# A running log-sum-exp: row sums in fp32 on GpSimd and VectorE, one fp32 triangular matmul, and a carry moved by a shuffle

## The chip, the cores and the metric

The kernel runs on one core of one Trainium2 chip. The metric is the device time of one execution in microseconds. The time before the change is 1263.03 us, the median of 10 runs that lie between 1262.51 and 1263.69.

## The reference

The input `x` has shape (4, 4096, 4128) in fp32: four batches, 4096 rows in time, 4128 independent columns. The output is the running log-sum-exp along the rows:

```
out[:, 0, :] = x[:, 0, :]
for t in range(1, S):
    mx = maximum(out[:, t - 1, :], x[:, t, :])
    out[:, t, :] = mx + log(exp(out[:, t - 1, :] - mx) + exp(x[:, t, :] - mx))
```

Both kernels compute the same thing without the maximum: the exponential of every element, a running sum over the rows of a batch, and the logarithm of that sum. Every element is read once and written once, 270.53 MB each way.

## The kernel before, in words

**Tiles.** A batch of 4096 rows is cut into steps (class `Step`) of 128 x 3 = 384 rows, with one step of 256 rows over; in batch 0 that small step comes first, in the others last. There are 44 steps, numbered 0 to 43 here: 40 of three rows a partition, 4 of two. In a step, partition p holds r = 3 (or 2) consecutive rows next to each other, so a tile `xt` is [128, r, 4128] fp32. Four such buffers exist (`bufs = 4`).

**Chunks.** Each tile is cut into four chunks of 1024 columns (class `Chunk`); the last chunk of a tile also takes the 32 columns that remain, the tail.

**What a chunk does.** `exp` (L128, ScalarE) writes the exponentials as fp16 over the tile itself. `head` (matmuls, all at L88, TensorE) fills a PSUM tile `pt` of [128, 1024]: for row 0 of each partition it multiplies with the triangular matrix `incl` (own partition and all above), for the rows 1 and 2 with `excl` (all partitions above), and it adds the running sum of the tiles before with `pick` from an fp16 carry tile that has a high and a low part. The PSUM now holds the sums for row 0. `stage(j)` takes the logarithm of `pt` into row j of the tile (L162, ScalarE) and then adds row j + 1 with two more matmuls against `ident`. After the last row `keep` (L92 and L93, VectorE) copies the last quadrant of `pt` as high and low fp16 parts into the carry of this chunk. The tail has its own PSUM tile `qt`, its own matmuls and one logarithm (L167).

**What sets the order.** The order is written out by hand (`manual_schedule`): each engine does its instructions in the order in which the program issues them. Round g of the main loop issues stage 2 of chunk g-2, stage 1 of chunk g-1 and stage 0 of chunk g, then the exponential of chunk g+2 and the head of chunk g+1. So ScalarE's queue holds the exponentials of the next tile ahead of the last logarithms of the present one. When the last stage of a tile's last chunk is issued, the store of the tile goes on SyncE's queue (L116), and behind it the load (L113) of the tile three steps ahead (`ahead = bufs - 1`). That load goes into the buffer of the tile before the one stored, and waits for that tile's store to have landed. Ahead of the loop three loads are issued.

Of the kernel before, what the change touches and what calls it, by code (L numbers as in the profile page):

```python
# [6 lines left out]

FP32 = mybir.dt.float32
FP16 = mybir.dt.float16
ACT = mybir.ActivationFunctionType  # L10
P = 128
R = 3
CH = 1024
MM = 512
HI, LO = 96, 32


def _constants(nc, pool):


    def tri(base, name):
        t = pool.tile([P, P], FP16, name=name)
        nc.gpsimd.memset(t, 1.0)

        nc.gpsimd.affine_select(  # L25
            out=t, in_=t, pattern=[[1, P]], compare_op=mybir.AluOpType.is_ge,
            fill=0.0, base=base, channel_multiplier=-1,
        )
        return t

    def ones_where_zero(bases, step, name):
        t = pool.tile([P, P], FP16, name=name)
        nc.gpsimd.memset(t, 0.0)
        for base in bases:
            nc.gpsimd.affine_select(  # L35
                out=t, in_=t, pattern=[[step, P]], compare_op=mybir.AluOpType.not_equal,
                fill=1.0, base=base, channel_multiplier=1,
            )
        return t

    return (
        tri(0, "incl"),
        tri(-1, "excl"),
        ones_where_zero([0], -1, "ident"),
        ones_where_zero([-(HI + 31), -(LO + 31)], 0, "pick"),
    )


@with_exitstack
def kernel(  # L50
    ctx: ExitStack,
    tc: tile.TileContext,
    x: bass.AP,
    out: bass.AP,
):

    nc = tc.nc
    B, S, D = x.shape
    assert S % P == 0
    n_main = D // CH
    tail = D - n_main * CH
    t0 = n_main * CH
    last = n_main - 1

    nc.scalar.preload_act_table_set("natural_log_exp_and_others")  # L70
    consts = ctx.enter_context(tc.tile_pool(name="consts", bufs=1))
    incl, excl, ident, pick = _constants(nc, consts)

    bufs = 4
    xpool = ctx.enter_context(tc.tile_pool(name="xpool", bufs=bufs))
    cpool = ctx.enter_context(tc.tile_pool(name="cpool", bufs=1))
    pmain = ctx.enter_context(tc.tile_pool(name="pmain", bufs=3, space=bass.MemoryType.PSUM))
    ptail = ctx.enter_context(tc.tile_pool(name="ptail", bufs=2, space=bass.MemoryType.PSUM))

    carry = [cpool.tile([P, CH], FP16, name=f"carry{c}") for c in range(n_main)]  # L80
    carry_t = cpool.tile([P, tail], FP16, name="carry_t")
    for t in (*carry, carry_t):
        nc.vector.memset(t, 0.0)  # L83

    ctx.enter_context(tc.manual_schedule())

    def mm(pt, w, rhs, start=False, stop=False):
        nc.tensor.matmul(pt, lhsT=w, rhs=rhs, start=start, stop=stop, skip_group_check=True)  # L88

    def keep(cr, pt):  # L90

        nc.vector.tensor_copy(cr[HI:HI + 32, :], pt[HI:HI + 32])  # L92
        nc.vector.tensor_tensor(  # L93
            out=cr[LO:LO + 32, :], in0=pt[HI:HI + 32], in1=cr[HI:HI + 32, :],
            op=mybir.AluOpType.subtract,
        )

    class Step:


        def __init__(self, b, row, r):
            self.b, self.row, self.r = b, row, r
            self.first = row == 0

        def dram(self, t):
            rows = t[self.b, self.row:self.row + P * self.r, :]
            return rows.rearrange("(p j) d -> p j d", j=self.r)

        def load(self):
            full = xpool.tile([P, R, D], FP32, name="xt")  # L110
            self.xt = full[:, :self.r, :]
            self.half = self.xt.bitcast(FP16)
            nc.sync.dma_start(out=self.xt, in_=self.dram(x))  # L113

        def store(self):
            nc.sync.dma_start(out=self.dram(out), in_=self.xt)  # L116

    class Chunk:
        def __init__(self, step, c):
            self.t, self.c = step, c  # L120
            self.w = D - last * CH if c == last else CH

        def e(self, j, a, b):
            return self.t.half[:, j, 2 * self.c * CH + a:2 * self.c * CH + b]

        def exp(self):
            c0, w = self.c * CH, self.w
            nc.scalar.activation(  # L128
                self.t.half[:, :, 2 * c0:2 * c0 + w], self.t.xt[:, :, c0:c0 + w], ACT.Exp,
            )  # L130

        def head(self):
            t = self.t
            pt = self.pt = pmain.tile([P, CH], FP32, name="pt")
            for j in range(t.r):
                for s in range(0, CH, MM):
                    mm(pt[:, s:s + MM], excl if j else incl, self.e(j, s, s + MM), start=j == 0)
            if not t.first:
                for s in range(0, CH, MM):
                    mm(pt[:, s:s + MM], pick, carry[self.c][:, s:s + MM])  # L140
            if self.c == last:
                self.tail_head()

        def tail_head(self):


            t, r = self.t, self.t.r
            full = ptail.tile([P, R, tail], FP32, name="qt")
            qt = self.qt = full[:, :r, :]
            to = lambda v, n: v.unsqueeze(1).to_broadcast([P, n, tail])  # L150
            for i in range(r):
                e = self.e(i, CH, CH + tail)
                mm(qt[:, i:, :], incl, to(e, r - i), start=i == 0)
                if i:
                    mm(qt[:, :i, :], excl, to(e, i))
            if not t.first:
                mm(qt, pick, to(carry_t, r))

        def stage(self, j):

            t, c, pt = self.t, self.c, self.pt
            nc.scalar.activation(t.xt[:, j, c * CH:(c + 1) * CH], pt, ACT.Ln)  # L162
            if j + 1 < t.r:
                for s in range(0, CH, MM):
                    mm(pt[:, s:s + MM], ident, self.e(j + 1, s, s + MM), stop=j + 2 == t.r)
                if c == last and j == 0:
                    nc.scalar.activation(t.xt[:, :, t0:D], self.qt, ACT.Ln)  # L167
                    keep(carry_t, self.qt[:, t.r - 1, :])
            else:
                keep(carry[c], pt)  # L170

    steps = []
    for b in range(B):
        n = S // P
        parts = [R] * (n // R) + ([n % R] if n % R else [])
        if b == 0:
            parts.reverse()
        row = 0
        for r in parts:
            steps.append(Step(b, row, r))  # L180
            row += P * r
        assert row == S

    chunks = [Chunk(s, c) for s in steps for c in range(n_main)]
    ahead = bufs - 1
    for s in steps[:ahead]:
        s.load()
    stored = 0
    chunks[0].exp()
    chunks[1].exp()  # L190
    chunks[0].head()
    for g in range(len(chunks) + R - 1):
        for d in range(R - 1, -1, -1):
            if 0 <= g - d < len(chunks) and d < chunks[g - d].t.r:
                k = chunks[g - d]
                k.stage(d)
                if k.c == last and d + 1 == k.t.r:
                    k.t.store()
                    if stored + ahead < len(steps):
                        steps[stored + ahead].load()  # L200
                    stored += 1
        if g + 2 < len(chunks):
            chunks[g + 2].exp()
        if g + 1 < len(chunks):
            chunks[g + 1].head()


# [28 lines left out]
```

## Time and profile before

| | |
|---|---|
| median of 10 runs | 1263.03 us |
| the profiled execution, its own time | 1262.96 us |
| its span | 1261.2 us |
| ScalarE busy | 947.1 us |
| TensorE matmuls busy | 690.2 us |
| VectorE busy | 451.4 us |
| GpSimd busy | 2.2 us |
| load of a three-row tile (6192 KB), issue to landing, median | 42.2 us |
| store of a three-row tile, issue to landing, median | 28.0 us |
| mean granted TensorE clock | 0.772 |

The page gives for each group of instructions the line, the engine (PE is TensorE, DVE is VectorE, ACT is ScalarE, POOL is GpSimd, SP is SyncE), the operation, what is written from what, the count, and then the busy time with the mean of one, and the idle time of the engine ahead of it with what ended that. A timeline row has start, duration, engine, line, and the idle time before it in brackets. A busy engine is not a bound in itself: what counts is which wait ends last in a stage.

### The profile page before, as it was taken

To read this page: it belongs to the slowest core of one execution; us is meant where nothing else is said; L and a number is where in the kernel's file an instruction comes from. 1 tells how busy PE (TensorE), PEld (TensorE's weight loads), DVE (VectorE), ACT (ScalarE), POOL (GpSimd) and SP (SyncE) were. 2 spreads that over 40 slices of the span, in tenths; PEclk is the share of its full clock that TensorE was granted. 3 is DMA by queue.
4 is the path that set the end of the run, shared out by engine and by line. 5 is a ranking of instruction groups with operands and counts; after the bars stand their busy time and mean duration, and the time that the engine had idled before them with its cause. 6 is when DMAs were issued, how large, how long until landed. Compare 5 with 4: busy or idle time off the path is not lost.

```text
span 1261.2 us, 6165 instructions
## 1 busy us (share of the span) xinstructions
PE 690.2 (55%) x2268; PEld 236.3 (19%) x2268; DVE 451.4 (36%) x445; ACT 947.1 (75%) x733; POOL 2.2 (0%) x13
## 2 busy tenths in 40 slices
PE   3665554556565555565346555555535765555552
PEld 1222111112121121221112121111211221111110
DVE  2443333333333333334424333333442433333344
ACT  5997777777777777778569777777966977777794
POOL 0000000000000000000000000000000000000000
PEclk9997777777677777777768777787776777778786
DMA  9999999999999999999999999999999999999998
GB/s 411 410 435 436 428 427 436 434 430 430 436 437 429 434 435 433 430 430 436 436 428 436 434 431 434 437 430 432 435 430 435 435 430 430 436 434 432 433 422 350
DMA packets 12702, 541.46 MB, mean 429 GB/s; under 512 B 1408, under 2 KB 1408, under 8 KB 1408
## 3 DMA queue, kind: packets, MB, share of 16 engines
q1 hardware_dynamic: 12672, 541.07, 99.5%
q8 instruction: 18, 0.29, 0.1%
q14 instruction: 12, 0.10, 0.0%
HBM read 270.53 MB, written 270.53 MB: 429 GB/s over the span
## 4 chain that ended last, share of the span: by engine, by line
DMA 69%; ACT 22%; PE 5%; issue 2%; DVE 1%; SPq 0%; ACTq 0%
DMA xt<-in_x_dram 67%; ACT xt L128 11%; ACT xt L162 10%; PE pt L88 5%; DMA out_dram<-xt 2%; ACT xt L167 0%; SPq L116 0%; DVE carry L92 0%; DVE carry L93 0%; ACTq L231 0%; SPq L113 0%; ACTq L128 0%; PE qt L88 0%
## 5 line engine op out<-in xcount | busy, mean ns | idle before, releaser
L128 ACT ACTIVATE xt<-xt 128x3072 f16<-128x3072 f32 (+3 forms) x176 | 478.3, 2717 | 248.1 <-DMA xt<-in_x_dram 248.1
L88 PE MATMUL pt<-xt,ident 128*128 128x512 f16 x672 | 250.7, 470 | 529.3 <-ACT xt L162 529.2
L162 ACT ACTIVATE xt<-pt 128x1024 f32<-128x1024 f32 x512 | 487.5, 1029 | 2.5 <-PE pt L88 0.7
L92 DVE CAST carry<-pt 32x1024 f16<-32x1024 f32 x176 | 216.4, 1230 | 761.3 <-ACT xt L162 761.0
L88 PE MATMUL pt<-xt,excl 128*128 128x512 f16 x672 | 247.0, 504 | 0.0
L93 DVE TENSOR_TENSOR carry<-pt,carry 32x1024 f16<-32x1024 f32 x176 | 215.8, 1226 | 6.1
L88 PEld LDWEIGHTS <-ident 128*128 128x128 f16 x672 | 70.3, 105 | 677.0 <-issue 653.3
L88 PE MATMUL pt<-xt,incl 128*128 128x512 f16 x352 | 151.8, 525 | 23.8 <-ACT xt L128 15.1
L88 PEld LDWEIGHTS <-excl 128*128 128x128 f16 x756 | 91.8, 123 | 141.3 <-issue 108.6
L88 PE MATMUL pt<-carry,pick 128*128 128x512 f16 x320 | 111.7, 436 | 0.0
L88 PEld LDWEIGHTS <-incl 128*128 128x128 f16 x480 | 45.2, 111 | 131.3 <-DVE carry L93 95.1
L88 PEld LDWEIGHTS <-pick 128*128 128x128 f16 x360 | 40.5, 113 | 56.8 <-issue 33.9
L167 ACT ACTIVATE xt<-qt 128x96 f32<-128x96 f32 (+1 forms) x44 | 10.9, 248 | 45.9 <-PE pt L88 45.9
L92 DVE CAST carry_t<-qt 32x32 f16<-32x32 f32 x44 | 8.7, 197 | 25.5 <-ACT xt L167 25.3
L88 PE MATMUL qt<-xt,incl 128*128 128x64 f16 (+2 forms) x128 | 12.7, 199 | 0.0
L88 PE MATMUL qt<-xt,excl 128*128 128x64 f16 (+1 forms) x84 | 10.7, 188 | 0.0
L93 DVE TENSOR_TENSOR carry_t<-qt,carry_t 32x32 f16<-32x32 f32 x44 | 8.5, 193 | 1.5
L88 PE MATMUL qt<-carry_t,pick 128*128 128x96 f16 (+1 forms) x40 | 8.3, 207 | 0.0
L83 DVE MEMSET carry<- 128x512 uint32 x4 | 1.9, 485 | 1.1 <-PEq L220 1.0
L70 ACT ACT_TABLE_LOAD x1 | 1.3, 1283 | 0.8 <-PEq L220 0.8
L35 POOL TENSOR_SCALAR_AFFINE_SELECT pick<-pick 128x128 f16<-128x128 f16 x2 | 0.6, 292 | 0.1
L25 POOL TENSOR_SCALAR_AFFINE_SELECT incl<-incl 128x128 f16<-128x128 f16 x1 | 0.3, 292 | 0.0
(11 smaller groups left out, 1.9 us busy)
## 6 DMA issues: line engine op xcount, KB each, us to landing
xt<-in_x_dram SPq DMA_DIRECT2D x40, 6192.0 KB, 42.2
out_dram<-xt SPq DMA_DIRECT2D x40, 6192.0 KB, 28.0
xt<-in_x_dram SPq DMA_DIRECT2D x4, 4128.0 KB, 37.2
out_dram<-xt SPq DMA_DIRECT2D x4, 4128.0 KB, 22.9
```

Of the source, the lines that this page charges most:

```text
L25: nc.gpsimd.affine_select(out=t, in_=t, pattern=[[1, P]], compare_op=mybir.AluOpType.is_ge, fill=0.0, base=base, channel_multiplier=-1,)
L35: nc.gpsimd.affine_select(out=t, in_=t, pattern=[[step, P]], compare_op=mybir.AluOpType.not_equal, fill=1.0, base=base, channel_multiplier=1,)
L70: nc.scalar.preload_act_table_set("natural_log_exp_and_others")
L83: nc.vector.memset(t, 0.0)
L88: nc.tensor.matmul(pt, lhsT=w, rhs=rhs, start=start, stop=stop, skip_group_check=True)
L92: nc.vector.tensor_copy(cr[HI:HI + 32, :], pt[HI:HI + 32])
L93: nc.vector.tensor_tensor(out=cr[LO:LO + 32, :], in0=pt[HI:HI + 32], in1=cr[HI:HI + 32, :], op=mybir.AluOpType.subtract,)
L128: nc.scalar.activation(self.t.half[:, :, 2 * c0:2 * c0 + w], self.t.xt[:, :, c0:c0 + w], ACT.Exp,)
L162: nc.scalar.activation(t.xt[:, j, c * CH:(c + 1) * CH], pt, ACT.Ln)
L167: nc.scalar.activation(t.xt[:, :, t0:D], self.qt, ACT.Ln)
```

## The change

All fp16 goes; everything is fp32 and stays in the tile. A chunk of a tile of r rows is now done so:

- `act(Exp)`: the exponential over the chunk's r rows, in place (ScalarE).
- `begin` (except in a batch's first tile): VectorE adds the carry, the running sum of all tiles before, to row 0 of partition 0. The instruction covers 32 partitions and multiplies the carry by `one`, which is 1 in partition 0 and 0 in the other 31.
- `own`: GpSimd adds row j-1 to row j in each partition, r - 1 instructions. (The change's own words give this sum to VectorE; the code issues it on `nc.gpsimd`.) Afterwards the last row of a partition holds the sum of its rows.
- `head`: two fp32 matmuls of 512 columns (and one of 32 for the tail) of the last row with `excl` give in PSUM, for each partition, the sum over all partitions above it.
- `add_before`: one VectorE instruction adds that PSUM tile to all r rows (a broadcast); one more does the tail.
- `end` (except in a batch's last tile): a VectorE `stream_shuffle` copies partition 127's last row of the chunk into all 32 partitions of the carry. The carry of chunk 0 lies in PSUM, those of the chunks 1 to 3 in SBUF.
- `act(Ln)`: the logarithm over the r rows with the tail, in place (ScalarE).

Round g issues the exponential of chunk g+3, `begin` and `own` of g+2, `head` of g+1, the logarithm of chunk g-1, then `add_before` and `end` of chunk g. The store of a tile follows its last logarithm. Four loads are issued ahead of the loop; the first store brings no load, and from the second store on each store is followed by the load three steps ahead, as before. The last step is a loop of its own, so none of its instructions is issued before all of the other 43 steps are. `hpool` holds two PSUM tiles for `head` (three `pt` before).

```diff
+    excl = pool.tile([P, P], FP32, name="excl")
...
+    one = pool.tile([Q, 1], FP32, name="one")
...
+    carry = [psum.tile([Q, CH], FP32, name="carry0")]
+    carry += [cpool.tile([Q, CH if c < last else D - last * CH], FP32, name=f"carry{c}")
+              for c in range(1, NC)]
...
+    def add(eng, o, a, b):
+        eng.tensor_tensor(out=o, in0=a, in1=b, op=mybir.AluOpType.add)
...
+        def act(self, func):
+            v = self.t.xt[:, :, self.a:self.b]
+            nc.scalar.activation(v, v, func)
+
+        def begin(self):
+
+            t = self.t
+            if not t.first:
+                v = t.xt[:Q, 0, self.a:self.b]
+                nc.vector.scalar_tensor_tensor(
+                    out=v, in0=carry[self.c], scalar=one, in1=v,
+                    op0=mybir.AluOpType.mult, op1=mybir.AluOpType.add,
+                )
+
+        def own(self):
+
+            x = self.t.xt
+            for j in range(1, self.t.r):
+                v = x[:, j, self.a:self.b]
+                add(nc.gpsimd, v, x[:, j - 1, self.a:self.b], v)
 
         def head(self):
...
+            e = t.xt[:, t.r - 1, self.a:self.b]
+            self.pt = hpool.tile([P, CH], FP32, name="pt")
+            parts = [(self.pt[:, s:s + MM], e[:, s:s + MM]) for s in range(0, CH, MM)]
             if self.c == last:
...
+                self.qt = psum.tile([P, tail], FP32, name="qt")
+                parts.append((self.qt, e[:, CH:]))
+            for o, v in parts:
+                nc.tensor.matmul(o, lhsT=excl, rhs=v, start=True, stop=True)
+
+        def add_before(self):
+            t = self.t
+            parts = [(t.xt[:, :, self.a:self.a + CH], self.pt)]
+            if self.c == last:
+                parts.append((t.xt[:, :, t0:], self.qt))
+            for v, p in parts:
+                add(nc.vector, v, v, p.unsqueeze(1).to_broadcast(v.shape))
+
+        def end(self):
+            t = self.t
+            if not t.final:
+                nc.vector.stream_shuffle(
+                    carry[self.c], t.xt[P - Q:, t.r - 1, self.a:self.b], [Q - 1] * Q,
+                )
...
-    for s in steps[:ahead]:
+    for s in steps[:bufs]:
         s.load()
     stored = 0
...
+    def result(k):
+        nonlocal stored
+        k.act(ACT.Ln)
+        if k.c == last:
+            k.t.store()
+            if bufs <= stored + ahead < len(steps):
+                steps[stored + ahead].load()
+            stored += 1
+
+
+    for part in (steps[:-1], steps[-1:]):
+        chunks = [Chunk(s, c) for s in part for c in range(NC)]
+        N = len(chunks)
+        for g in range(-3, N + 1):
+            if 0 <= g + 3 < N:
+                chunks[g + 3].act(ACT.Exp)
+            if 0 <= g + 2 < N:
+                chunks[g + 2].begin()
+                chunks[g + 2].own()
+            if 0 <= g + 1 < N:
+                chunks[g + 1].head()
+            if 0 <= g - 1:
+                result(chunks[g - 1])
+            if 0 <= g < N:
+                chunks[g].add_before()
+                chunks[g].end()
```

## The prediction

> **What bounds the kernel now.** I read the page first: busy shares, slices, queues, chain.
>
> ```profile
> span 1261.2 us, 6165 instructions
> PE 690.2 (55%) x2268; PEld 236.3 (19%) x2268; DVE 451.4 (36%) x445; ACT 947.1 (75%) x733; POOL 2.2 (0%) x13
> ...
> DMA  9999999999999999999999999999999999999998
> ...
> q1 hardware_dynamic: 12672, 541.07, 99.5%
> ...
> DMA 69%; ACT 22%; PE 5%; issue 2%; DVE 1%; SPq 0%; ACTq 0%
> ```
>
> The 16 DMA engines are full in every slice but the last; no compute engine passes 75%. The chain is loads (67%) joined by short pieces of ScalarE. So the transfers set the pace, and a change can cost time only by letting the DMA run dry. How far is it from that? SyncE's timeline of two tiles, then ScalarE's and SyncE's at the end (the last row merges three stores, issued at 1212.2, 1233.8 and 1244.4):
>
> ```profile
> 722.71 0.34 SPq L116 DMA_DIRECT2D out_dram<-xt  x1
> 723.14 0.38 SPq L113 DMA_DIRECT2D xt<-in_x_dram  x1
> 751.95 0.34 SPq L116 DMA_DIRECT2D out_dram<-xt  x1
> ```
>
> ```profile
> 1196.39 2.76 ACT L128 ACTIVATE xt<-xt 128x3072 f16<-128x3072 f32 x1 [6.16 <-DMA xt<-in_x_dram]
> ...
> 1220.98 1.91 ACT L128 ACTIVATE xt<-xt 128x2048 f16<-128x2048 f32 x1 [1.34 <-DMA xt<-in_x_dram]
> ```
>
> ```profile
> 1182.81 0.34 SPq L116 DMA_DIRECT2D out_dram<-xt  x1
> 1183.25 0.38 SPq L113 DMA_DIRECT2D xt<-in_x_dram  x1
> 1212.22 32.54 SPq L116 DMA_DIRECT2D out_dram<-xt  x3
> ```
>
> A three-row tile takes 29.3 us (722.7 to 752.0): one load and one store at 14.65 us each. ScalarE waits 6.2 us for tile 42 (landed 1196.4), and tile 41's store goes out 15.8 us later, at 1212.2, because ScalarE's queue holds three exps of tile 42 ahead of tile 41's last logs. I call this delay, landing of the next tile to store, L. At landing only one load (14.65 us, issued with the previous store) and that store are still queued, 29.3 us of work; so with L = 15.8 us about 13.5 us of cover remain, and the DMA runs dry in mid-run only if L exceeds 29.3 us.
>
> The costs of single instructions:
>
> ```profile
> L128 ACT ACTIVATE xt<-xt 128x3072 f16<-128x3072 f32 x120 | 332.0, 2767 | 233.3 <-DMA xt<-in_x_dram 233.3
> L128 ACT ACTIVATE xt<-xt 128x3168 f16<-128x3168 f32 x40 | 115.5, 2886 | 0.0
> L128 ACT ACTIVATE xt<-xt 128x2048 f16<-128x2048 f32 x12 | 22.9, 1912 | 14.8 <-DMA xt<-in_x_dram 14.8
> ```
>
> ```profile
> L93 DVE TENSOR_TENSOR carry<-pt,carry 32x1024 f16<-32x1024 f32 x176 | 215.8, 1226 | 6.1
> L93 DVE TENSOR_TENSOR carry_t<-qt,carry_t 32x32 f16<-32x32 f32 x44 | 8.5, 193 | 1.5
> ```
>
> VectorE: (1226 - 193) / 992 = 1.04 ns an element after 160 ns.
>
> **What the Trainium skill says.** "VectorE: DVE Perf Modes", the perf-mode tier table: an fp32 tensor_tensor has no faster mode, 2293 ns for 2048 elements, and a shuffle of [32, 2048] about 2400 ns. My line gives 2290 ns: the trace agrees. "GPSIMD Engine Reference", 3.1: a GpSimd fp32 add of 2048 takes 4497 ns; no row of this trace shows one. "SBUF — State Buffer", Who interferes with whom: a VectorE instruction with two SBUF inputs and a GpSimd one that reads SBUF lock each other out for whole instructions; one with a PSUM input does not. Nothing here shows it. "FP8 and Floating Point Precision", TensorE Precision Notes: true fp32 is four passes; not shown here.
>
> **The change part by part,** for a three-row tile, against 29.3 us.
>
> *ScalarE.* Four exps as before. The logs, twelve from PSUM at 1.029 us, become four over 3072 or 3168 elements; I price them like the exps: 2.77. Exps and logs together: 2 x (3 x 2.77 + 2.89) = 22.4 us. Beside the transfers, except in L.
>
> *VectorE.* `keep` goes (two at 1.23 a chunk). `begin` adds 1.23, `end` 1.25 (the shuffle), `add_before` 3072 elements: 0.16 + 3072 x 1.04 ns = 3.36, and 0.26 for the tail. A tile: 4 x 5.84 + 0.3 = 23.7, about 24 with gaps; bounds 23 and 26. Whole run some 980 us. Covered; if the cover went, the tile would take these 24 us plus what it waits for. The set-up memsets that go (1.9 us) lay before the first landing: nothing.
>
> *GpSimd.* `own`: two adds of 1024 a chunk. The page's 4497 ns less 0.1 fixed (its one-element memset takes 98 ns here) halves to 2.2, plus 0.1: 2.3 us. From below, the trace's one-input select of 128 elements (292 ns) gives 1.5 ns an element, 1.6 us; from above I allow 3.3. `begin` reads the carry from SBUF in three of four chunks, and is locked against `own`; `own` in turn waits for its `begin`. So they alternate: 1.23 + 2 x 2.3 + two hand-overs of 0.1 = 6.0 us a chunk, 24 a tile. Behind a waiting `begin` on VectorE stand `add_before` and `end` (4.6 us), which fit beside the next `own` (4.6). Covered, with 5 us left.
>
> *TensorE.* Twelve 512-column matmuls a chunk fall to two, nine matmuls a tile with the tail (should the 18 in the change's words count halves, the work is the same). In the last tile, two pairs:
>
> ```profile
> 1233.61 1.06 PE L88 MATMUL pt<-carry,pick 128*128 128x512 f16 x2
> ...
> 1239.60 0.59 PE L88 MATMUL pt<-xt,ident 128*128 128x512 f16 x2 [1.75 <-ACT xt L162]
> ```
>
> A single one takes 378 ns where a pair takes 0.59 us, so a second pass adds 0.21; the slower granted clock gives 0.63 and 1.06, so 0.43. The page's four passes for each of two matmuls make eight: 1.9 to 3.6 us a head. I take 2.6. Covered in mid-run.
>
> *Order of the queues, mid-run.* In round g ScalarE does exp(g+3), then log(g-1). Tile k's last log now stands behind all four exps of tile k+1: L = four exps and four logs = 22.4 us. VectorE's `begin` of tile k+1 also blocks `add_before` of tile k's third chunk until the first exp; then 2.8 + 1.2 + 3.4 = 7.4 us after landing, well before the log that needs it (11). So L = 22.5 and cover falls from 13.5 to 6.8 us. It costs nothing while L stays below 29.3; the next load waits for the previous store on SyncE's queue, which lands some 7 us before. Cost: 0 (bounds 0 and +3, since the 16 engines don't run level: from 1230 to 1235 us they moved 211 GB/s, a part of them dry before store 42 came).
>
> *Start.* Four loads are issued at once, but no load goes with store 0. Loads land at 13.2, 27.8, and by 14.65 steps 42.4 and 57.1; store 0 (9.8 us) would end at 66.9. ScalarE reaches store 0 four rounds after tile 1's landing, 27.8 + 4 x 4.75 = 46.8 (exp 2.8, log 1.95), and store 1 four full rounds later, 69.2. A transfer into an empty queue costs more: the first load took 13.18 - 0.80 = 12.4 for 9.8 of work, so 2.6. The queue is dry for 69.2 + 2.6 - 66.9 = 4.9 us; fast engines are dry sooner, slow ones later. Before, store 1 (63.7) and load 3 met no gap. I take +4 (bounds 0 and +10, the latter with GpSimd adds of 2.9).
>
> *End.* The last tile is now a pipeline of its own: its first exp stands behind tile 42's last log. Tile 42 lands at 1196.4 + 4 = 1200.4. Its fourth `begin` ends some 22 us after landing (2.8 for the first exp, three rounds of 6, its own 1.2); VectorE still has three `add_before` and two `end`: 3 x 3.36 + 0.3 + 2 x 1.25 = 12.9, so 35, less the 0.8 by which the first rounds run ahead of 6; the last log ends at 37 and store 42 goes at 1237.5 (before: 1233.8). Then exp 1.9, begin 1.2, one GpSimd add 2.3, head 2.6, add_before 2.3, log 1.9 and hand-overs 0.4 make 12.6 us to the first chunk's result, three more at 3.7 and a tail 0.3: 24 us, store 43 at 1261.5 (before 1244.4). Store 42 ends 17 us after its issue, so the queue is dry about 8 us. The last store needs 9.8 + 2.6 = 12.4: landing 1273.9, and 0.8 to the end of the span as now: 1274.7. Bounds on this part: last tile 20 to 28, drain 32 to 41.
>
> **Sum.** 1261.2 + 4 (start) + 0 (mid-run) + 9.5 (end) = 1274.7 of span; 1.8 lies around the span (1262.96 - 1261.2), so 1276.5. That execution is 0.07 us from the median of 1263.03. Forecast: 1276, its own range 1267 to 1288.
>
> **Rivals.** (A) *GpSimd and the lock become the pace.* Decides at an add of (29.3 / 4 - 1.23 - 0.2) / 2 = 2.95 us. At 3.3 a chunk takes 8.0 us, a full tile 32, and 40 full tiles 1280, four small ones 19 each and 30 of fill and drain: about 1385. For it: no row shows the price. Against: the stated price has 28% to spare. (B) *Not slower.* The dry spell at the start falls into slack of the slow engines (cost 0), and a last tile of 19 us after a drain of 31 us brings the last store out at 1196.4 + 31 + 19 = 1246.4, end 1246.4 + 12.4 + 0.8 + 1.8 = 1261.4. It decides if GpSimd's add is nearer 1.6 and TensorE's head 1.9 us. Against: the last tile starts only after the drain, whatever the adds cost. (C) *The words rather than the diff*: with the row sums on VectorE, 8 x 1.23 more a tile is 33.5 us; 40 x 33.5 and four small tiles of 24, with fill and drain, some 1450. The diff has them on GpSimd.
>
> **Chances.** Forecast 0.70, A 0.17, B 0.11, C 0.02. The range leaves out the upper part of A, C and the lower part of B: 1262 to 1310. About 0.2% (1260.5 to 1265.6) is what a measurement of this kernel can tell from no change: faster 0.05, same 0.07, slower 0.88.
>
> **What would show it.** DMA slices still full in mid-run, with one dip near 65 to 72 us and one of 8 us before the last store; ScalarE idle at every landing, stores 22 to 23 us after it; GpSimd adds of 2.2 to 2.4 us; VectorE near 980 us. If ScalarE no longer waits for loads, or GpSimd's adds pass 2.9 us, A holds and I am wrong; if store 1 leaves before 66 us, the start term is.

## The result, and the profile after

The changed kernel takes 1293.59 us (median of 8 runs, 1292.55 to 1295.46), against 1262.96 us before: ratio 1.0245, 95% interval 1.0237 to 1.0254. It is 30.6 us slower; the forecast had 13. The profiled execution, the fastest of them, took 1292.55 us with a span of 1290.4.

The page of the changed kernel, the lines that answer to those shown of before:

```profile
span 1290.4 us, 3961 instructions
PE 607.3 (47%) x792; PEld 212.1 (16%) x792; DVE 990.9 (77%) x700; ACT 920.9 (71%) x353; POOL 799.9 (62%) x344
...
q1 hardware_dynamic: 12672, 541.07, 98.1%
...
DMA 54%; ACT 23%; DVE 12%; issue 8%; POOL 1%; PE 1%; SPq 1%; ACTq 0%; DVEq 0%
```

Still no compute engine is full, and the same 541.07 MB move. But the DMA's share fell from 99.5% to 98.1%, and its share of the chain from 69% to 54%.

The groups of the changed kernel, shapes apart (count, then busy time and mean ns of one, then the idle time before them):

```profile
L107 ACT ACTIVATE xt<-xt 128x3072 f32<-128x3072 f32 x240 | 643.2, 2750 | 328.4 <-DMA xt<-in_x_dram 320.9 <-DVE carry L149 7.5
L136 PE MATMUL pt<-xt,excl 128*128 128x512 f32 x704 | 597.7, 1000 | 666.7 <-POOL xt L78 658.0 <-DVE xt L78 8.5 <-issue 0.2
L78 POOL TENSOR_TENSOR xt<-xt 128x1024 f32<-128x1024 f32 x252 | 596.1, 2367 | 419.6 <-DVE xt L114 366.0 <-ACT xt L107 44.2
L78 DVE TENSOR_TENSOR xt<-xt,pt 128x3072 f32<-128x3072 f32 x160 | 533.5, 3335 | 40.9 <-PE pt L136 32.1 <-issue 8.7
L114 DVE SCALAR_TENSOR_TENSOR xt<-carry,one,xt 32x1024 f32<-32x1024 f32 x120 | 159.1, 1327 | 209.0 <-ACT xt L107 206.4
L149 DVE STREAM_SHUFFLE carry<-xt 32x1024 f32<-32x1024 f32 x120 | 152.4, 1270 | 1.6
```

Most durations are near their forecasts: logarithms and exponentials 2.75 us (forecast 2.77), GpSimd's adds 2.37 (2.3), `add_before` 3.34 (3.36), the shuffle 1.27 (1.25), `begin` 1.33 (1.23). The matmuls appear as two records each of 1.0 us, 18 a tile. One price is off: the four records of a head take 3.7 us from the first start to the last end (median of 176), where 2.6 was forecast with 3.6 as the upper bound. TensorE waits 658 us for GpSimd and is off the path in mid-run, so it is not a price of an engine's work that failed.

Where did the time go? I take as a tile's landing the start of its first exponential, where ScalarE's timeline shows it waiting for the load. Tile 4 lands at 100.24 us before and 103.39 after; tile 42 at 1196.39 and 1215.95. That cuts the extra 29.2 us of span in three:

| part | before | after | more | forecast |
|---|---|---|---|---|
| start, to the landing of tile 4 | 100.2 | 103.4 | 3.2 | 4 |
| mid-run, landing of tile 4 to that of tile 42 | 1096.2 | 1112.6 | 16.4 | 0 |
| end, from there to the end of the span | 64.8 | 74.5 | 9.6 | 9.5 |

Start and end came as forecast; mid-run lost what was to cost nothing. The landing of tile 41 on ScalarE and the store of tile 40 on SyncE, in the changed kernel:

```profile
1186.65 21.50 ACT L107 ACTIVATE xt<-xt 128x3072 f32<-128x3072 f32 x8 [7.67 <-DMA xt<-in_x_dram]
```

```profile
1208.17 0.33 SPq L98 DMA_DIRECT2D out_dram<-xt  x1
1208.60 0.38 SPq L95 DMA_DIRECT2D xt<-in_x_dram  x1
```

The store follows the landing by 21.5 us (15.8 before, forecast 22.5): eight activations. The changed kernel in stretches of 3 us around the two-row tile 21 (from the left: the length, then the busy times of PE, PEld (weight loads), DVE, ACT and POOL, the granted clock, and last the DMA share and GB/s; a packet counts whole where it starts, so a full stretch can show 0.94 or 1.02):

```profile
591.00:594.00 3.00, 3.00 (x4) 0.93 (x4) 3.00 (x2) 3.00 (x2) 1.95 (x1) 0.51 1.02 440
594.00:597.00 3.00, 0.41 (x2) 0.10 (x1) 2.91 (x4) 3.00 (x2) 2.77 (x2) 1.00 0.46 198
597.00:600.00 3.00, 3.00 (x4) 0.86 (x4) 3.00 (x2) 0.23 (x1) 1.96 (x1) 0.56 0.99 424
678.00:681.00 3.00, 2.81 (x4) 0.67 (x2) 3.00 (x2) 3.00 (x3) 2.62 (x2) 0.50 0.76 330
681.00:684.00 3.00, 0.85 (x1) 0.50 (x2) 2.91 (x4) 2.50 (x1) 2.10 (x1) 0.50 0.50 215
```

SyncE in the same kernel:

```profile
597.25 0.33 SPq L98 DMA_DIRECT2D out_dram<-xt  x1
...
683.52 0.33 SPq L98 DMA_DIRECT2D out_dram<-xt  x1
```

The DMA falls to half just ahead of store 19 (597.25) and of store 22 (683.52). Those are the two stores ahead of which a two-row transfer stands in the queue: the load of tile 21 and the store of tile 21. In the kernel before, the stretches ahead of the same two stores (584.86 and 669.16) are full:

```profile
582.00:585.00 3.00, 1.90 (x8) 0.80 (x9) 0.14 (x1) 3.00 (x3) 0.00 (x0) 1.00 0.94 407
...
666.00:669.00 3.00, 3.00 (x10) 1.10 (x9) 0.27 (x1) 3.00 (x3) 0.00 (x0) 0.66 0.99 429
```

In long stretches, cut at the landings of tiles 4, 20, 26, 31, 36 and 42, the changed kernel shows:

```profile
103.40:575.70 472.30, 227.32 (x291) 78.99 (x290) 370.69 (x260) 343.97 (x128) 304.11 (x128) 0.60 1.00 432
575.70:748.10 172.40, 82.51 (x110) 28.46 (x109) 127.82 (x90) 122.11 (x48) 104.47 (x44) 0.62 0.98 414
748.10:895.30 147.20, 69.93 (x91) 24.36 (x90) 118.61 (x85) 107.49 (x40) 95.06 (x40) 0.60 1.01 434
895.30:1037.40 142.10, 68.81 (x94) 24.32 (x92) 104.00 (x73) 100.61 (x40) 85.48 (x36) 0.62 0.98 410
1037.40:1215.90 178.50, 84.08 (x106) 29.23 (x107) 142.33 (x102) 128.98 (x48) 114.10 (x48) 0.61 1.00 432
```

Only the two stretches that hold a two-row tile (21 and 32) are below 1.00. The kernel before has in the first of them:

```profile
569.00:736.10 167.10, 89.03 (x297) 30.86 (x297) 61.29 (x60) 125.72 (x98) 0.00 (x0) 0.77 1.00 433
```

**The theory (cover).** The later store leaves the DMA queue too little to do: most of all where a two-row tile stands in it. **Rivals.** Pace: the GpSimd adds and their lock with VectorE make the rounds long. Traffic: the fp32 work, GpSimd's above all, slows the transfers themselves.

### The profile page after: what moved, and what is told of

It reads as the page before. It is cut to its first block, busy times and chain, and to the rows that moved or that the text cites. A ratio compares the mean times of both kernels' runs of the same rounds, so it can differ in the third digit from the quotient of the medians.

```text
span 1290.4 us, 3961 instructions
## 1 busy us (share of the span) xinstructions
PE 607.3 (47%) x792; PEld 212.1 (16%) x792; DVE 990.9 (77%) x700; ACT 920.9 (71%) x353; POOL 799.9 (62%) x344
## 3 DMA queue, kind: packets, MB, share of 16 engines
q1 hardware_dynamic: 12672, 541.07, 98.1%
## 4 chain that ended last, share of the span: by engine, by line
DMA 54%; ACT 23%; DVE 12%; issue 8%; POOL 1%; PE 1%; SPq 1%; ACTq 0%; DVEq 0%
DMA xt<-in_x_dram 54%; ACT xt L107 23%; DVE xt L78 7%; DVE xt L114 3%; DVE carry L149 2%; POOL xt L78 1%; PE pt L136 1%; SPq L98 0%; ACTq L107 0%; SPq L95 0%; DVEq L78 0%; DVEq L114 0%; DVEq L221 0%
## 5 line engine op out<-in xcount | busy, mean ns | idle before, releaser
L107 ACT ACTIVATE xt<-xt 128x3072 f32<-128x3072 f32 (+3 forms) x352 | 919.6, 2691 | 356.7 <-DMA xt<-in_x_dram 337.7
L78 POOL TENSOR_TENSOR xt<-xt 128x1024 f32<-128x1024 f32 (+1 forms) x336 | 799.1, 2379 | 470.9 <-DVE xt L114 413.5
L136 PE MATMUL pt<-xt,excl 128*128 128x512 f32 x704 | 597.7, 1000 | 666.7 <-POOL xt L78 658.0
L78 DVE TENSOR_TENSOR xt<-xt,pt 128x3072 f32<-128x3072 f32 (+1 forms) x176 | 569.8, 3239 | 66.3 <-PE pt L136 57.4
L114 DVE SCALAR_TENSOR_TENSOR xt<-carry,one,xt 32x1024 f32<-32x1024 f32 (+1 forms) x160 | 217.2, 1358 | 210.2 <-ACT xt L107 206.4
L136 PEld LDWEIGHTS pt<-xt,excl 128*128 128x128 f32 x704 | 185.8, 291 | 1021.3 <-POOL xt L78 857.5
L149 DVE STREAM_SHUFFLE carry<-xt 32x1024 f32<-32x1024 f32 (+1 forms) x160 | 205.9, 1287 | 2.1
L136 PEld LDWEIGHTS qt<-xt,excl 128*128 128x128 f32 x88 | 26.3, 299 | 40.4 <-issue 40.4
L136 PE MATMUL qt<-xt,excl 128*128 128x32 f32 x88 | 18.0, 294 | 0.0
L78 DVE TENSOR_TENSOR xt<-xt,qt 128x96 f32<-128x96 f32 (+1 forms) x44 | 10.2, 233 | 0.0
## 6 DMA issues: line engine op xcount, KB each, us to landing
out_dram<-xt SPq DMA_DIRECT2D x40, 6192.0 KB, 22.5
```

The lines of the kernel that those rows point to most:

```text
L78: eng.tensor_tensor(out=o, in0=a, in1=b, op=mybir.AluOpType.add)
L107: nc.scalar.activation(v, v, func)
L114: nc.vector.scalar_tensor_tensor(out=v, in0=carry[self.c], scalar=one, in1=v, op0=mybir.AluOpType.mult, op1=mybir.AluOpType.add,)
L136: nc.tensor.matmul(o, lhsT=excl, rhs=v, start=True, stop=True)
L149: nc.vector.stream_shuffle(carry[self.c], t.xt[P - Q:, t.r - 1, self.a:self.b], [Q - 1] * Q,)
```

## The experiments

### The logarithm first: the delay cut in the changed kernel

```diff
         for g in range(-3, N + 1):
+            if 0 <= g - 1:
+                result(chunks[g - 1])
             if 0 <= g + 3 < N:
                 chunks[g + 3].act(ACT.Exp)
...
-            if 0 <= g - 1:
-                result(chunks[g - 1])
```

> The changed kernel with one edit: in each round the logarithm of chunk g-1 is issued ahead of the exponential of chunk g+3, so that a tile's last logarithm stands behind three exponentials of the next tile and not four. Nothing else moves; VectorE, GpSimd and TensorE keep their work and order. Cover theory (the 16 us lost in mid-run come from the store leaving 21.5 us after the next tile's landing, which leaves the DMA queue too little): that delay falls to 16.6 us, the mid-run loss from 16 to 2 us or less, and the start's 3 us go too, since store 1 leaves at 65 us; 1274 to 1278 us. Pace theory (GpSimd's adds and their lock with VectorE make the rounds long) and traffic theory (the fp32 work slows the transfers themselves): the mid-run loss stays, 1289 to 1293 us.

Measured: 1283.71 us, ratio to before 1.0165 (1.0149 to 1.0180). Ten us less than the changed kernel, all in mid-run: its loss falls from 16.4 to 6.7 us; start 103.7 and end 74.1 stay. That is more than pace or traffic alone had (1289 to 1293) and less than cover had (1274 to 1278). ScalarE and SyncE of this kernel show a part of the reason:

```profile
1177.33 8.07 ACT L107 ACTIVATE xt<-xt 128x3072 f32<-128x3072 f32 x3 [5.54 <-DMA xt<-in_x_dram]
1186.14 5.42 ACT L107 ACTIVATE xt<-xt 128x3072 f32<-128x3072 f32 x2 [0.74 <-DVE carry L149]
1192.35 5.58 ACT L107 ACTIVATE xt<-xt 128x3168 f32<-128x3168 f32 x2 [0.79 <-POOL xt L78]
```

```profile
1195.22 0.33 SPq L98 DMA_DIRECT2D out_dram<-xt  x1
```

The delay is 17.9 us and not 16.6: ScalarE now reaches a logarithm before VectorE has the sum. Store 1 stayed at 69.4 us, so at the start it isn't ScalarE that sets the rounds, as I had worked out; the run without GpSimd's adds shows below who does.

### The delay lengthened in the kernel before

```diff
-        if g + 2 < len(chunks):
-            chunks[g + 2].exp()
+        if g + 3 < len(chunks):
+            chunks[g + 3].exp()
```

(and a third exponential ahead of the loop.)

> The kernel before with one edit: the exponentials run three chunks ahead and not two. No GpSimd adds, no fp32 matmul, VectorE unchanged. Cover theory: the delay from landing to store rises from 15.8 to about 22.5 us, and mid-run loses 12 to 20 us as in the changed kernel; with some 5 us more at the end, where tile 42 waits for four exponentials of the last tile: 1278 to 1288 us. Pace and traffic theories: nothing in mid-run, only the end's 5 us: 1263 to 1268 us.

Measured: 1278.84 us, 1.0124 (1.0107 to 1.0141). This kernel has no GpSimd add, no fp32 matmul and VectorE at 451 us, and it loses 10.0 us in mid-run with a delay of 20.9 us, and 4.6 at the end:

```profile
1178.11 2.76 ACT L128 ACTIVATE xt<-xt 128x3072 f16<-128x3072 f32 x1 [6.64 <-DMA xt<-in_x_dram]
```

```profile
1198.99 0.34 SPq L116 DMA_DIRECT2D out_dram<-xt  x1
```

The kernel before is made slow by nothing but an exponential issued a chunk earlier. Pace and traffic had 1263 to 1268. The time lies in the cover theory's span, but the mid-run loss is below its 12 to 20.

### GpSimd's adds left out

```diff
                 chunks[g + 2].begin()
-                chunks[g + 2].own()
```

> The changed kernel without GpSimd's adds: the rows of a partition are not summed, so GpSimd is idle, its lock with VectorE never held, and nothing else is left out. Cover theory: ScalarE's order is untouched, the delay stays 21.5 us and mid-run still loses 14 to 17 us; only the drain and the last tile get shorter, by 3 to 8 us together: 1285 to 1290 us. Pace theory: the mid-run loss goes, 1268 to 1274 us. Traffic theory: it falls in part.

Measured: 1283.60 us, 1.0163 (1.0148 to 1.0178). The sums of a partition's rows are missing from this kernel's result; the rest of the work is there. The delay stays 21.5 us, and mid-run still loses 11.6 in the profile: pace as the main cause falls. The profiled execution was the fastest of four, 2.4 us below the median, so the usual loss is nearer 14 (an estimate that puts all of the 2.4 into mid-run), the lower edge of the cover theory's 14 to 17. GpSimd's part is worked out below from the medians. Tile 4 lands at 100.5: the start's 3 us go with `own`, whose alternation with `begin` had set the rounds; store 1 leaves at 67.4. The end falls to 70.2.

The same cut in the log-first kernel:

> The log-first kernel without GpSimd's adds: the rows of a partition are not summed, nothing else is left out. The end falls by about 4 us as it did without the adds before. Cover alone: the delay is 16.6 to 17.9 us, mid-run loses what the log-first kernel lost less what the shorter delay gives, 5 to 7 us: 1277 to 1280 us. Cover and GpSimd as separate parts: mid-run loses 1 to 3 us: 1272 to 1276 us.

Measured: 1272.96 us, 1.0074 (1.0059 to 1.0089), mid-run loss 4.8. Log first takes 9.9 us off with the adds and 10.6 without, the adds 10.0 and 10.7: two separate parts.

### The last step in the common loop

```diff
-    for part in (steps[:-1], steps[-1:]):
+    for part in (steps,):
```

> The changed kernel with the last step back in the common loop, so that its exponentials run beside the last work of tile 42. All theories: store 42 leaves some 3 us later (behind the last tile's exponentials), the last store some 8 us earlier, then right behind store 42 in the queue; end 4 us earlier, 1288 to 1291 us, mid-run untouched. If the end's 9.6 us come from something other than the split, no change.

Measured: 1288.28 us, 1.0206 (1.0190 to 1.0221). The end falls from 74.5 to 69.2 us, 5.3 less: the split of the last step makes over half of the end's loss. With the log first as well:

> The changed kernel with both edits that have helped: the logarithm first in the round, and the last step in the common loop. If the mid-run part and the end are separate parts of the loss, the gains add: 1293.6 less 9.9 less 5.3 is 1278.4; 1276 to 1280 us. The start's 3 us stay. No theory has it at the 1263 us of the kernel before.

Measured: 1278.00 us, 1.0118 (1.0102 to 1.0135): the gains add. It is the best form of the changed kernel that computes everything, and slower than before.

### VectorE's sums ahead of the next tile: a miss

```diff
-            if 0 <= g + 2 < N:
-                chunks[g + 2].begin()
-                chunks[g + 2].own()
...
             if 0 <= g < N:
                 chunks[g].add_before()
                 chunks[g].end()
+            if 0 <= g + 2 < N:
+                chunks[g + 2].begin()
+                chunks[g + 2].own()
```

> The log-first kernel with one more edit: VectorE does add_before and end of chunk g ahead of begin (and GpSimd's own) of chunk g+2, so that tile k's sums no longer stand behind the next tile's landing. Landing to store falls from 17.9 to about 16.5 us. Cover alone: with 16.5 us mid-run loses 1 us or less against the kernel before, 1277 to 1280 us. Cover and GpSimd (the adds cost some 5 us in mid-run whatever the delay): mid-run still loses 4 to 6 us, 1281 to 1284 us. The start and the end's 9 us stay in both.

> The add-first kernel with the last step in the common loop as well. The end falls from 74 us after the landing of tile 42 to about 69, as it did in the one-loop kernel: 5 us below the add-first kernel, 1272 to 1279 us. No theory has it below the 1263 of the kernel before, whose end is 64.8 us.

Measured: 1295.15 us, 1.0254 (1.0238 to 1.0269), and with one loop 1287.45, 1.0189 (1.0174 to 1.0204). They lie 11 and 8 us above the upper ends of what I expected. The waits of the add-first kernel (in total, times, longest):

```profile
DVE xt L78 <- PE pt L136: 210.0, 77, 21.4
...
ACT xt L107 <- DMA xt<-in_x_dram: 158.4, 32, 11.0
```

In the changed kernel these two are:

```profile
ACT xt L107 <- DMA xt<-in_x_dram: 337.7, 41, 13.7
...
DVE xt L78 <- PE pt L136: 57.4, 9, 21.1
```

With `begin` at the end of the round, the way through `own` and `head` to the next but one `add_before` no longer fits beside VectorE's other work: VectorE waits for `head` 77 times, 2.7 us on average. The profile shows where that costs time. From tile 11 to 19 the store leaves 16.2 us after the landing, as expected, and hardly anything is lost; but stores 3 to 10 leave 20 to 27 us after it, and mid-run loses 8.5 us in all, 6.7 of them before tile 12 lands. The larger part of the miss is the end: 86.8 us, where the log-first kernel has 74.1 (with one loop 79.1 against 68.6). There no transfer covers the chain of engines, and ScalarE waits 3 to 6 us for VectorE or GpSimd ahead of most logarithms. This is rival A of the prediction at the start and the end of the run, reached by the order of one queue and not by the price of an add.

### Does GpSimd slow the transfers, and by what?

Seven adds of 256 elements a chunk in a spare tile, in the kernel before, waited for by nobody:

```diff
+    spare = cpool.tile([P, 256], FP32, name="spare")
+    nc.gpsimd.memset(spare, 0.0)
...
+        for _ in range(7):
+            nc.gpsimd.tensor_tensor(out=spare, in0=spare, in1=spare, op=mybir.AluOpType.add)
```

> The kernel before with GpSimd kept busy: seven adds of 256 fp32 elements a chunk in a tile of its own, some 4.6 us a chunk as in the changed kernel, on data that nothing else uses and with no wait between GpSimd and the others, so that it runs on its own for the first 700 to 900 us. ScalarE's order and the delay of 15.8 us are untouched. Cover alone: no change, 1262 to 1264 us. If GpSimd's traffic slows the transfers: 3 to 6 us more, all of it while GpSimd is busy, 1266 to 1269 us.

Measured: 1265.82 us (13 runs), 1.0023 (1.0014 to 1.0031): 2.8 us more, a little under the span expected, while the delay is untouched at 15.8. Its trace loses 3.5 us in mid-run, and only 0.3 of it in the eleven tiles after GpSimd has done (at 862 us). Then 42 adds of 8 elements in their place:

```diff
-        for _ in range(7):
+        for _ in range(42):
```

(and the spare tile [128, 8].)

> The kernel before with 42 adds of 8 fp32 elements a chunk on GpSimd in a tile of its own, in place of seven adds of 256: six times as many instructions and a thirtieth part of the data. With seven adds of 256 the kernel took 2.8 us more, and its trace has ten more 8 KB packets of the instruction queue than that of the kernel before. If a GpSimd instruction costs by its fetch through the DMA engines: some 58 packets at 0.28 us each, 12 to 18 us more, 1275 to 1281 us. If it costs by the data that GpSimd reads and writes: nothing measurable, 1262 to 1264 us.

Measured: 2074.19 us, 1.640 (1.636 to 1.644), which says nothing by itself: each small add takes 197 ns, and GpSimd is still busy with them some 780 us after the last store has landed. What can be compared is the landing of tile 42: 1214.2 us, and mid-run 18.7 us longer than before. The DMA queues that carry instructions (packets, MB), in the kernel before, with seven adds, and with 42:

```profile
q8 instruction: 18, 0.29, 0.1%
q14 instruction: 12, 0.10, 0.0%
```

```profile
q8 instruction: 18, 0.29, 0.1%
q14 instruction: 22, 0.18, 0.0%
```

```profile
q14 instruction: 71, 0.58, 0.1%
q8 instruction: 18, 0.29, 0.1%
```

One of these adds has a thirtieth of the elements of one before. By the landing of tile 42 GpSimd had done 4402 of them, 3.5 times the 1246 of the other run, with a ninth of its elements in all, and they cost five times the time: it isn't GpSimd's data. In mid-run the first run has 9 packets more on the instruction queue than the kernel before, the second 32 more (43 against 11): 0.4 to 0.6 us each.

The traces also place them. In the first run six of the sixteen tiles from 13 to 28 have one more 8 KB packet between their landing and the next: 13, 16, 19, 22, 25 and 28. Exactly these take 0.65 to 0.67 us longer than before; of the ten others nine are within 0.02 us of it, and one (21) is 1.45 us shorter. So the added packet and the added time fall in the same tile. How it comes to cost 0.66 us, when its own record lasts 0.31, no run shows.

### The changed kernel again, and the two-row tile moved

> The changed kernel itself once more, for a second profile: 1292 to 1296 us. It shows how much the mid-run loss of one execution (16 us in the first) and its share around the two-row tiles (10 us) vary: by 3 us at most if the cover sets them.

Measured, a single execution: 1294.91 us, mid-run loss 18.6, of it 8.7 between the landings of tiles 20 to 26 and 31 to 36 (10.0 in the first profile). The one-loop kernel, whose mid-run is the same, has 19.5 in its profile. So a difference of three us between single profiles is no finding.

```diff
-        if b == 0:
+        if b in (0, 1):
             parts.reverse()
```

> The changed kernel with batch 1 cut the other way round: its two-row tile comes first (tile 11) and not last (tile 21). Work, queues and order in a round are the same. Cover theory: the 5 us that were lost between the landings of tiles 20 and 26 move with the two-row tile to the landings of tiles 10 to 16, the second loss (tiles 31 to 36) stays, and the time stays at 1292 to 1296 us. If the losses come from the boundary between two batches or from the place in time, they stay between tiles 20 and 26.

Measured: 1290.70 us, 1.0221 (1.0204 to 1.0238), about a microsecond under the span expected. The six tiles 10 to 16, which now hold the two-row tile, take 171.4 us; six tiles with one took 167.1 before: a loss of 4.3. Tiles 20 to 26, now all of three rows, take 176.8, against 175.5 for six such tiles before: 1.3 where 5.3 had been. In this kernel:

```profile
300.00:303.00 3.00, 0.66 (x1) 0.00 (x0) 3.00 (x2) 3.00 (x2) 2.88 (x2) 0.50 0.51 220
...
681.00:684.00 3.00, 2.69 (x4) 1.06 (x4) 3.00 (x2) 0.65 (x1) 1.81 (x2) 0.58 1.07 462
```

The dip now stands ahead of store 9 (303.37), the first with the two-row load in front of it, and at 681 us the DMA is full. The loss follows the small tile.

### The runs side by side

The packet records of the traces tell two more things. Each transfer is spread over 16 engines, and these don't finish together: the **spread** is the time from the first to the last engine's end of one transfer, here the load of tile 21. And the **dry time** is the time for which an engine had no packet, as the mean of the 16, here around store 19. When store 19 comes, the first engine to finish still has 24.4 us of work less the delay less the spread; this is what is **left**.

| kernel | delay, us | spread | left | dry at store 19 | mid-run loss | of it at the two-row tiles |
|---|---|---|---|---|---|---|
| before, seven adds of 256 | 15.8 | 6.3 | 2.3 | 0.0 | 3.5 | 0.1 |
| log first, no adds | 17.8 | 5.0 | 1.6 | 0.0 | 4.8 | 1.8 |
| log first | 17.9 | 5.6 | 0.9 | 0.1 | 6.7 | 2.6 |
| before, exponentials three ahead | 20.9 | 4.0 | -0.5 | 0.5 | 10.0 | 6.5 |
| changed, no adds | 21.5 | 4.3 | -1.4 | 1.4 | 11.6 | 6.8 |
| before, 42 adds of 8 | 15.8 | 10.7 | -2.1 | 1.3 | 18.7 | 6.8 |
| changed | 21.5 | 5.2 | -2.3 | 2.0 | 16.4 | 10.0 |

The part at the two-row tiles is that between the landings of tiles 20 and 26 and of 31 and 36. The dry time rises as what is left falls (1.4 and 1.3 us are the one exception). The delay is the larger part of it but not the only one: 42 small adds leave the delay at 15.8 us and widen the spread to 10.7, and the engines run dry as well.

In the changed kernel the engines were dry for 6.1 us of mid-run, all of it at the two-row tiles, and their packets took 10.2 us longer than before: together 16.3, the whole loss. Of the 10.2 us, 7.5 fall in the tiles right behind the dips (21, 24, 32 and 35), and in the kernel with the two-row tile moved 7.4 in 11, 14, 32 and 35: they follow the small tile too. Why packets take longer there, no run shows; log first without adds has 3.8 us of it in the same four tiles, with hardly an engine dry.

## Why the prediction was wrong

The direction was right, and so was the rise of the delay; the size was not: 1276 us forecast with a range of its own to 1288, 1293.6 measured. The largest cost, 16.4 us of 29.2, had been put at 0.

**The step that failed** is "Order of the queues, mid-run", the term that ends in a cost of 0 with bounds 0 and +3. It measured 16.4 us (18.6 and 19.5 in the two other profiles with the same mid-run). It saw the delay rise and the cover shrink, and then took the cover of a three-row tile for all of them, and 16 engines that don't run level for a matter of 3 us at most. Around a two-row tile the queue holds 14.65 + 9.77 = 24.4 us after a landing, not 29.3; less the delay of 21.5 that leaves 2.9 us. A store into an empty queue also starts late: the last one of this kernel took 11.2 us for 9.8 of work, so it lost 1.4 (I had 2.6, from the first load). And the engines end the load of tile 21 5.2 us apart. So the first of them run dry while the last are still at work. Two such tiles stand in mid-run, with two thin places each: 8.7 to 10 us lost in four dips and behind them.

At three-row tiles 29.3 - 21.5 = 7.8 us remain, more than the spread, and there the DMA is full (1.00, 1.01 and 1.00 in the three long stretches). The other 6.4 us are lost with all engines busy. A part is longer packets, 1.9 us. For the rest the landings give a hint: a tile has landed when the last engine is done. The dips bring the engines together (the spread falls from 5.2 to 0.9 us by store 22, and from 4.1 to 1.1 by store 33), and in the tiles that follow they drift apart again, to 4.2 and 4.5. That this makes up the rest is argued, not shown.

**GpSimd's part** had no term. I priced its adds and the lock, not what its instructions cost the DMA. The pairs of profiles with and without the adds give 4.8 and 2.0 us of mid-run, where single profiles of one kernel differ by three. The medians, less what the profiles show for start and end, give about 3 in both pairs (10.0 - 2.9 - 4.3 and 10.7 - 3.5 - 3.8). The changed kernel has 14 packets on the instruction queue in mid-run, without the adds 10; four at 0.66 us would be 2.6, an estimate from the run with seven adds.

**Start:** +4 forecast, 3.2 measured, by luck: the reason is another than mine. Store 1 left at 69.4 us (69.2 forecast), but ScalarE alone would have it at 67.4; `begin` and `own`, at 5.9 us a round, set it. My 22.4 us for eight activations was some 4% long: they take 21.5 in a row.

**End:** +9.5 forecast, 9.6 measured. Store 42 came 39.5 us after the landing (37 forecast), store 43 another 23.0 later (24), the end 12 after that (13.2). That the sum came out is luck in part: errors of +2.5, -1.0 and -1.2 us cancel. The one-loop run shows 5.3 us of it to be the split.

**The prices** held but for the head, and so did two of the Trainium skill's pages behind them. The estimate of 2.3 us from "GPSIMD Engine Reference", 3.1, stands against 2.37 measured. The lock of "SBUF — State Buffer", Who interferes with whom, shows in `begin` (min, median, max ns), with the adds and without:

```profile
L114 DVE SCALAR_TENSOR_TENSOR xt<-carry,one,xt x160: 1268/1274/3030, 30.5 to 1267.2; 32x1024 f32<-32x1024 f32 x120, 32x1056 f32<-32x1056 f32 x40
```

```profile
L114 DVE SCALAR_TENSOR_TENSOR xt<-carry,one,xt x160: 1270/1273/1307, 30.6 to 1256.3; 32x1024 f32<-32x1024 f32 x120, 32x1056 f32<-32x1056 f32 x40
```

Five of 160 take 1.76 to 3.03 us; each of these began while a GpSimd add had 0.65 to 1.95 us to go, and ended 1.1 us after it. Most others begin in the last 0.3 us of an add and take 0.13 us more at most, and the 40 whose carry lies in PSUM never exceed 1.28 (only five of these meet an add at all). In all `begin` is busy for 217.2 us with the adds and 204.8 without. So the lock is there and costs VectorE 12 us in the whole run.

**The rivals.** A (pace) did not come: ScalarE still waits 337.7 us for loads, and the adds stay below 2.95. B (not slower) asked for a drain of 31 us and a last tile of 19; they took 39.5 and 23.0. C (the words rather than the diff) is ruled out by 336 adds on GpSimd.

**What stays open:** why packets take longer behind a dip, how the last 4 to 5 us at three-row tiles come about, and how an 8 KB packet of instructions comes to cost 0.66 us. I also did not try a form with more buffers.

## What to carry to other kernels

In a kernel bound by its transfers, work out for every store how much the queue still holds when it comes, for the smallest tile in the row and not for the usual one, and take off the time by which the DMA engines end apart (4 to 11 us here). Where 2.3 us were left no engine ran dry; where less than nothing was left, they did, although no compute engine was full. The order of one engine's queue sets that number: an exponential issued one chunk earlier cost the old kernel 16 us, 10 of them in mid-run, and a logarithm issued ahead of it gave the new one 10 back. And an engine with room to spare is not free: a reordering that shortens the delay can lengthen the chain between engines where no transfer covers it, as the add-first run did at its end.

## What the hardware showed that I had not expected

- GpSimd instructions that nobody waits for cost a kernel bound by its transfers 2.8 us in 1263 (interval 1.8 to 3.9): it goes with their number, not with their data. Tiles with one more 8 KB packet of the instruction queue took 0.66 us longer; over the whole of mid-run it is 0.4 to 0.6 us a packet.
- The 16 DMA engines drift apart as a kernel runs: the load of tile 21 ended over 5.2 us in the changed kernel and over 10.7 with 42 small GpSimd adds a chunk. When the queue runs dry they come together again, to about 1 us.
- The lock between GpSimd and VectorE stretched five of 160 `begin` from 1.27 us to as much as 3.03, and left the median as it was.
- An fp32 matmul of 512 columns shows as two records of 1.0 us. TensorE's granted clock is 0.616 on average, against 0.772 in the fp16 kernel, although TensorE is busy for less of the time.
